# Second block's attention: six of eight head pairs divide by their softmax sums on the finished head rows instead of on the probabilities

## The chip, the cores and the metric

The kernel runs on one core of one Trainium2 chip, as one program. The core's engines each work through their own instruction stream, in order: TensorE (PE: matmuls and transposes; PEld is its weight load), VectorE (DVE), ScalarE (ACT), GpSimd (POOL) and SyncE (SP, which issues DMA). The metric is the time of one execution in microseconds (us), lower is better, as a median of several executions.

## What is computed

Two transformer blocks follow each other, each with two layers, on 512 positions by 1024 features in float32. The change lies in the attention of the second block. Each of its layers has 16 heads of 64 columns: 6 "dilated" ones (kind A), 4 "differential" ones (kind B), 6 "latent" ones (kind C).

```
def causal_attention(q, k, v):                       # kind C
    ...
        s = jnp.einsum('bqhd,bkhd->bhqk', qs, k).astype(jnp.float32) * scale
        p = jax.nn.softmax(jnp.where(causal, s, -jnp.inf), axis=-1)
        return jnp.einsum('bhqk,bkhd->bqhd', p.astype(v.dtype), v)

def diff_attention(q1, q2, k1, k2, v, lam, bias_tab):  # kind B
    ...
        a = probs(q1, k1) - lam * probs(q2, k2)
        return jnp.einsum('bhqk,bkhd->bqhd', a.astype(v.dtype), v)

    # kind A: three dilated windows, mixed by their log-sum-exp
    w = jax.nn.softmax(jnp.stack(lses, axis=0), axis=0)
    o = jnp.sum(w[..., None] * jnp.stack(outs, axis=0).astype(jnp.float32), axis=0)

    o_b = (rms_norm(o_b, subln_g, SUBLN_EPS) * (1.0 - lam_init)).astype(x.dtype)
    heads = jnp.concatenate([o_a.reshape(Bn, S, -1), o_b..., o_c...], axis=-1)
    h = layer_norm(DEEPNORM_ALPHA * x + heads @ w_o, ln1_g, ln1_b)
```

The kernel computes kind A as one softmax over all causal positions with a bias table, which gives the same mixture. So each head is exp(scores) divided by its row sums, times V.

## The kernel before, in words

`second_mix` does one layer's attention in eight units, each a pair of heads, in the order `UNITS`: B0, C0, B1, C1, A0, C2, A1, A2. Every unit has three parts. `proj(i)` projects q, k and v (for kind C from the compressed tiles `ct`; else from the activations `xt`), with three matmuls (L212, L213, L214) for each product, since float32 is split into a high and a low part that the matmul can take. `att()` does the two heads. `fin()`, which before only kind B has, normalises the pair's rows.

The loop at the end of `second_mix` emits `proj(i+1)`, then, in a stretch of raised priority (`AHEAD` = 102), `att()` of unit i and `fin()` of unit i-1. A scheduler sorts all of it into one fixed stream for each engine by these priorities, so that projection matmuls of the next unit stand between the pieces of a head. At run time no engine passes its next instruction.

A head in `att2`: for four blocks of 128 query rows, PE forms scores in PSUM (`sps`, L1025), DVE adds the bias table and finds the row minimum (`L`, `nm`, L1028), ACT takes the exponential and the row sums (L1032). `L` holds the causal parts of the four blocks, 128, 256, 384 and 512 columns wide. Then DVE takes the reciprocal of the four sums (L1041) and multiplies the four parts by it (L1051). `finish()` transposes the probabilities (PE, `tps<-ident,L`, L1063), splits them into `pth` (ACT, L165) and `ptl` (DVE, L169), multiplies by V (PE, `pv`, L1079, L1080, L1077) and puts the result into the pair's rows `heads` (ACT L1089, DVE L1090). In `heads` the partitions are the pair's 128 head columns and the free axis is the 512 positions. V comes from `vpair`: ACT copies the projection (L996), PE transposes it (L999), ACT and DVE split it (L1003, L1004).

Kind B combines two softmaxes on the probabilities (L1053) and divides by the first one's sum at the end: its `fin()` squares the rows (ACT, L1164), sums them (PE, `half2`, L1167), takes the inverse root (POOL, L219, L222), spreads the resulting 128x8 numbers over 128x512 (DVE copy, L1175), transposes that (PE, L1180) and multiplies the rows by it (DVE, L1181).

After the eight units the out-projection multiplies `heads`, split into `ht`, by w_o. A few lines of the pools and of the loop:

```
UNITS = (("B", 0, 3), ("C", 0, 5), ("B", 1, 4), ("C", 1, 6), ("A", 0, 0), ("C", 2, 7), ("A", 1, 1), ("A", 2, 2))
            with self.tc.high_priority(offset=AHEAD):
                for finish in att():
                    finish()
                if fin is not None:
                    fin()
```

Of the kernel before, what the change touches and what calls it, by code (L numbers as in the profile page):

```python
# [9 lines left out]
F32 = mybir.dt.float32  # L10
F32R = mybir.dt.float32r
AF = mybir.ActivationFunctionType
ALU = mybir.AluOpType
# [3 lines left out]
P = 128  # L17
D = 1024
KT = D // P
SEQ = 512  # L20
CTX = 256
NX = SEQ // P
# [95 lines left out]
class _Kernel:  # L118
# [890 lines left out]

    def att2(self, pool, subs, T, V, par, dest, nlam=None, inv=None):  # L1010
        nc = self.nc
        Ps = []
        off = [0, P, 3 * P, 6 * P]
        for _ in subs:
            L = pool.tile([P, 10 * P], F32, tag="L", bufs=3, name="L")
# [23 lines left out]
        L, r = Ps[0]  # L1039
        if nlam is None:  # L1040
            nc.vector.reciprocal(r, r)  # L1041
        else:

            L2, r2 = Ps[1]
            nc.vector.reciprocal(r2, r2)
            nc.vector.scalar_tensor_tensor(r2, r2, nlam, r, op0=ALU.mult, op1=ALU.mult)
            nc.vector.reciprocal(inv, r)
        for i in range(NX):
            c = slice(off[i], off[i] + (i + 1) * P)
            if nlam is None:  # L1050
                nc.vector.tensor_scalar(L[:, c], L[:, c], r[:, i : i + 1], None, ALU.mult)  # L1051
            else:
                nc.vector.scalar_tensor_tensor(  # L1053
                    L[:, c], L2[:, c], r2[:, i : i + 1], L[:, c], op0=ALU.mult, op1=ALU.add
                )
# [38 lines left out]
    def second_mix(self, l, pool):  # L1094
        nc, A = self.nc, self.A
# [18 lines left out]
        nc.vector.tensor_scalar(sg, self.col[:, 102 + l : 103 + l], 1.0 - li, None, ALU.mult)  # L1114

        def dilated(p, o):
            Q, K, L = self.qk(pool), self.qk(pool), self.qk(pool)
# [5 lines left out]
            for j in range(2):  # L1123
# [3 lines left out]
                nc.gpsimd.tensor_copy(K[j][ro], K[j][r])  # L1127
            V = self.vpair(pool, self.proj_t(W, 768 + p * P))

            def att():  # L1130
                for j in range(2):
                    T = self.table(t2, 2 * p + j)
                    yield self.att2(t2, [[(Q[j], K[j]), (Q[j], L[j])]], T, V, j, o)

            return att, None

        def differential(p, o):
# [15 lines left out]
            V = self.vpair(pool, self.proj_t(W, b0 + 512))  # L1153
            inv = self.small(8, "inv", 2)

            def att():
                for j in range(2):
                    T = self.table(t2, 6 + 2 * p + j)
                    subs = [[(QK[0][i], QK[1][i])] for i in (2 * j, 2 * j + 1)]
                    yield self.att2(t2, subs, T, V, j, o, nlam=nlam, inv=inv[:, j:8:2])  # L1160

            def fin():
# [3 lines left out]
                for t in range(NX):  # L1166
# [7 lines left out]
                nc.vector.tensor_tensor(r8, r8, inv, op=ALU.mult)  # L1174
                nc.vector.tensor_copy(  # L1175
                    sq.rearrange("p (a b) -> p a b", b=64), r8.unsqueeze(2).to_broadcast([P, 8, 64])
                )
                tp = self.tps()
                for t in range(NX):
                    nc.tensor.transpose(tp[:, t * P : (t + 1) * P], sq[:, t * P : (t + 1) * P], self.ident)  # L1180
                nc.vector.scalar_tensor_tensor(o, o, sg, tp, op0=ALU.mult, op1=ALU.mult)  # L1181

            return att, fin

        def latent(p, o):
# [10 lines left out]
            for j in range(2):  # L1196
# [8 lines left out]
                qs.append((qh, ql))  # L1205

            def att():
                Tc = self.table(t2, 10)
                for j in range(2):
                    kh, kl = Kb[j]  # L1210
                    qh, ql = qs[j]
                    yield self.att2(t2, [[(qh, kh), (qh, kl), (ql, kh)]], Tc, V, j, o)

            return att, None

# [79 lines left out]
        fin = None  # L1295
        for i in range(len(UNITS)):
# [8 lines left out]
            fin = fn  # L1305
        assert fin is None
        t2.release()
# [189 lines left out]
```

## Time and profile before

| what | value |
|---|---|
| median of 3 runs | 2005.67 us (1997.89 to 2006.74) |
| the profiled execution, its own time | 2004.78 us |
| its span in the trace | 2003.0 us, mean granted PE clock 0.981 |
| PE, DVE, ACT, POOL busy | 1918.2, 1224.4, 895.0, 171.3 us |
| attention stretch of the second block, layer 0 | about 725 to 928 us |
| attention stretch of the second block, layer 1 | about 1350 to 1580 us |

The span is the part of the execution that the trace covers; the other 1.8 us lie around it. Busy shares are over the whole program; the attention stretches have their own, which the rows below show. A line number such as L1051 is the line in the kernel before. Behind the change the same code has other numbers: the transposes L1063 become L1058, the PV matmuls L1079, L1080, L1077 become L1074, L1075, L1072, the row add L1090 becomes L1085, L1167 becomes L1179.

### The profile page before, as it was taken

Reading aid. Unit: us, or ns where it says so; the run is one execution under the profiler, and the core shown is the slowest. Engines: PE = TensorE matmul, PEld = TensorE weight load, DVE = VectorE, ACT = ScalarE, POOL = GpSimd, SP = SyncE. Lnnn points to the kernel's source line nnn. Section 1 sums busy time; section 2 is a strip of 40 time slices with the busy share of each in tenths; the row PEclk is TensorE's granted clock in tenths of the full one; section 3 lists DMA queues with packets and bytes.
Section 4 is the critical chain, followed back from the end, with each engine's and each line's share of the span. In section 5 each row is a group of like instructions: output and inputs, shape, how many; then the busy total and the mean of one; then the engine's idle time right before and its main releaser. Section 6 shows DMA issues by size and latency. Waiting matters only on the chain.

```text
span 2003.0 us, 25662 instructions
## 1 busy us (share of the span) xinstructions
PE 1918.2 (96%) x9516; PEld 1571.8 (78%) x9516; DVE 1224.4 (61%) x2422; ACT 895.0 (45%) x1744; POOL 171.3 (9%) x299
## 2 busy tenths in 40 slices
PE   6999999999999998899999999999899999999997
PEld 4878888788787876777888888887677788888886
DVE  3759984475987668776733434367877673343434
ACT  4746662484654457665321322225756522132220
POOL 2100000030000121101100000012110110000001
PEclk9999999999999999999999999999889999999999
DMA  8414342142432341123432324324112343232421
GB/s 290 151 46 138 102 130 74 44 150 64 127 85 85 119 127 50 53 85 103 124 95 84 107 73 122 95 90 112 48 54 84 108 119 100 78 114 66 126 74 43
DMA packets 220449, 197.19 MB, mean 98 GB/s; under 512 B 30154, under 2 KB 178128, under 8 KB 220324
## 3 DMA queue, kind: packets, MB, share of 16 engines
q1 hardware_dynamic: 209940, 160.32, 27.4%
q0 software_dynamic: 10384, 35.24, 5.3%
q8 instruction: 75, 1.23, 0.3%
q14 instruction: 50, 0.41, 0.1%
HBM read 187.09 MB, written 12.03 MB: 99 GB/s over the span
## 4 chain that ended last, share of the span: by engine, by line
PE 81%; DVE 5%; ACT 5%; issue 2%; DMA 1%; POOL 1%; POOLq 0%; DVEq 0%; ACTq 0%; SPq 0%
PE acc L212 22%; PE acc L213 22%; PE acc L214 22%; PE sps L1025 2%; PE tps L1063 2%; PE tps L792 1%; PE pv L1079 1%; PE pv L803 1%; DVE wl L169 1%; ACT wh L165 1%; ACT L L1032 1%; PE pv L804 1%; PE pv L1080 1%; PE tps L410 1%; DMA wr<-in_w_mod_dram 1%
## 5 line engine op out<-in xcount | busy, mean ns | idle before, releaser
L165 ACT ACTIVATE wh<-wr 128x1024 fp32r<-128x1024 f32 (+3 forms) x299 | 311.7, 1045 | 608.1 <-PE acc L213 266.3
L169 DVE TENSOR_TENSOR wl<-wr,wh 128x1024 fp32r<-128x1024 f32 (+3 forms) x299 | 358.2, 1201 | 256.9 <-ACT wh L165 254.4
L212 PE MATMUL acc<-xt,wh 128*128 128x512 f32 (+1 forms) x1200 | 464.4, 387 | 1.2 <-DVE kb L169 0.7
L214 PE MATMUL acc<-xt,wl 128*128 128x512 f32 (+1 forms) x1200 | 463.7, 386 | 0.0
L213 PE MATMUL acc<-xt,wh 128*128 128x512 f32 (+1 forms) x1200 | 463.0, 386 | 0.0
L212 PEld LDWEIGHTS acc<-xt,wh 128*128 128x128 f32 x1200 | 226.4, 189 | 40.9 <-DVE kb L169 1.1
L214 PEld LDWEIGHTS acc<-xt,wl 128*128 128x128 f32 x1200 | 226.2, 189 | 39.8
L213 PEld LDWEIGHTS acc<-xt,wh 128*128 128x128 f32 x1200 | 226.1, 188 | 38.9 <-issue 0.2
L212 PE MATMUL acc<-wh,ht 128*128 128x512 f32 (+1 forms) x494 | 192.6, 390 | 0.0
L213 PE MATMUL acc<-wl,ht 128*128 128x512 f32 (+1 forms) x494 | 191.8, 388 | 0.0
L214 PE MATMUL acc<-wh,ht 128*128 128x512 f32 (+1 forms) x494 | 191.5, 388 | 0.1
L165 ACT ACTIVATE pth<-tps 128x384 fp32r<-128x384 f32 (+1 forms) x176 | 90.0, 536 | 109.8 <-PE tps L1063 54.3
L169 DVE TENSOR_TENSOR ptl<-tps,pth 128x384 fp32r<-128x384 f32 (+1 forms) x176 | 104.0, 613 | 30.4 <-ACT pth L165 29.6
L214 PEld LDWEIGHTS acc<-wh,ht 128*128 128x128 f32 x494 | 92.9, 188 | 21.8 <-DVE ht L169 1.0
L212 PEld LDWEIGHTS acc<-wh,ht 128*128 128x128 f32 x494 | 92.8, 188 | 20.6
L213 PEld LDWEIGHTS acc<-wl,ht 128*128 128x128 f32 x494 | 92.8, 188 | 20.1
L1418 DVE SCALAR_TENSOR_TENSOR h<-h,acc 128x512 f32<-128x512 f32 (+1 forms) x50 | 33.2, 664 | 114.4 <-PE acc L214 114.4
L1032 ACT ACTIVATE L<-L,nm 128x384 f32<-128x384 f32 (+3 forms) x160 | 88.9, 557 | 24.1 <-DVE nm L1028 23.5
L1384 DVE SCALAR_TENSOR_TENSOR th<-th,acc 128x512 f32<-128x512 f32 x42 | 28.9, 687 | 112.9 <-PE acc L214 112.6
L1028 DVE CUSTOM_DVE_ANT_0 L<-sps,T 128x512 f32<-128x512 f32 (+3 forms) x160 | 74.9, 486 | 26.1 <-PE sps L1025 24.7
L219 POOL TENSOR_SCALAR rv<-bna 128x1 f32<-128x1 f32 x16 | 18.8, 1173 | 792.0 <-DVE bna L1313 792.0
L214 PE MATMUL acc<-wh,xt 128*128 128x256 f32 (+2 forms) x256 | 84.9, 332 | 1.1 <-DVE xt L169 0.8
(315 smaller groups left out, 3390.4 us busy)
## 6 DMA issues: line engine op xcount, KB each, us to landing
wr<-in_w_in_dram SPq DMA_DIRECT2D x66, 512.0 KB, 4.8
wr<-in_w_gate_dram SPq DMA_DIRECT2D x44, 512.0 KB, 4.0
wr<-in_w_up_dram SPq DMA_DIRECT2D x44, 512.0 KB, 4.1
wr<-in_w_down_dram SPq DMA_DIRECT2D x42, 512.0 KB, 3.6
wr<-in_w_mod_dram SPq DMA_DIRECT2D x40, 512.0 KB, 4.5
wr<-in_w_o_dram SPq DMA_DIRECT2D x32, 256.0 KB, 2.7
T<-skew POOLq DMA_DIRECT2D x26, 256.0 KB, 3.1
x<-in_x_dram POOLq DMA_DIRECT2D x8, 512.0 KB, 6.8
```

Of the source, the lines that this page charges most:

```text
L165: self.nc.scalar.activation(out, in_, AF.Copy, scale=scale)
L169: self.nc.vector.tensor_tensor(out, in_, hi.bitcast(F32), op=ALU.subtract)
L212: mm(ps, lh, rh, start=(first and i == 0), stop=False)
L213: mm(ps, lh, rl, start=False, stop=False)
L214: mm(ps, ll, rh, start=False, stop=(last and i == n - 1))
L410: nc.tensor.transpose(v[:, k, :], src[:, (kb * 4 + k) * P : (kb * 4 + k + 1) * P], self.ident)
L1025: nc.tensor.matmul(ps[:, :w], x[:, tok], y[:, :w], start=(k == 0), stop=(k == len(s) - 1))
L1028: nc.vector.tensor_tensor_reduce(lc, ps[:, :n], T[:, SEQ - n : SEQ], 1.0, 3.0e38, op0=ALU.add, op1=ALU.min, accum_out=nm[:, i : i + 1],)
L1032: nc.scalar.activation(lc, lc, AF.Exp, bias=nm[:, i : i + 1], scale=-1.0, accum_out=sums[:, i : i + 1])
L1063: nc.tensor.transpose(tp[:, (i - j) * P : (i - j + 1) * P], L[:, off[i] + j * P : off[i] + (j + 1) * P], self.ident)
L1384: nc.vector.scalar_tensor_tensor(th, th, 0.5, pu, op0=ALU.mult, op1=ALU.mult)
L1418: nc.vector.scalar_tensor_tensor(h[:, c], h[:, c], ALPHA if gi == 0 else 1.0, ps, op0=ALU.mult, op1=ALU.add)
```

## The change

For kinds A and C the four multiplications of the probabilities (L1051) are gone: 4 for each head, 12 heads in a layer, two layers, 96 instructions. The reciprocal stays, and goes into `inv`, 8 columns for a pair. In their place a kind A or C unit gets a `fin()`: `by_row` spreads `inv` over 128x512 (DVE copy, L1113 behind the change), transposes it (four PE transposes, L1118) and multiplies the rows of the pair (DVE, L1120, from PSUM). Kind B calls the same `by_row`, which holds the code that stood in its own `fin()`. The last unit's `fin()` is called behind the loop, without the raised priority. `inv` has three buffers instead of two, and the spread numbers use the pool of `vt`.

```
-    def att2(self, pool, subs, T, V, par, dest, nlam=None, inv=None):
+    def att2(self, pool, subs, T, V, par, dest, inv, nlam=None):
...
-        if nlam is None:
-            nc.vector.reciprocal(r, r)
-        else:
-
+
+        nc.vector.reciprocal(inv, r)
+        if nlam is not None:
             L2, r2 = Ps[1]
             nc.vector.reciprocal(r2, r2)
             nc.vector.scalar_tensor_tensor(r2, r2, nlam, r, op0=ALU.mult, op1=ALU.mult)
-            nc.vector.reciprocal(inv, r)
-        for i in range(NX):
-            c = slice(off[i], off[i] + (i + 1) * P)
-            if nlam is None:
-                nc.vector.tensor_scalar(L[:, c], L[:, c], r[:, i : i + 1], None, ALU.mult)
-            else:
+            for i in range(NX):
+                c = slice(off[i], off[i] + (i + 1) * P)
                 nc.vector.scalar_tensor_tensor(
...
+        def by_row(o, r8, sg, sq):
+
+            nc.vector.tensor_copy(
+                sq.rearrange("p (a b) -> p a b", b=64), r8.unsqueeze(2).to_broadcast([P, 8, 64])
+            )
+            tp = self.tps()
+            for t in range(NX):
+                nc.tensor.transpose(tp[:, t * P : (t + 1) * P], sq[:, t * P : (t + 1) * P], self.ident)
+            if sg is None:
+                nc.vector.tensor_tensor(o, o, tp, op=ALU.mult)
+            else:
+                nc.vector.scalar_tensor_tensor(o, o, sg, tp, op0=ALU.mult, op1=ALU.mult)
...
-            return att, None
+            def fin():
+                by_row(o, inv, None, pool.tile([P, SEQ], F32, tag="vt", bufs=2, name="iv"))
+
+            return att, fin
...
-        assert fin is None
+        fin()
```

The scheduler sorts the streams anew, so more moves than the diff shows. The numbers behind the names are buffers of the built program and differ between the two kernels.

**Layer 0, DVE, the softmax of C0's first head.** `L_7818` holds its exponentials, the `qk` and `wl` rows are other work. Before:

```order
L1041 RECIPROCAL sum5_7820<-sum5_7820 128x4
L169 TENSOR_TENSOR wl_8242<-wr_8239,wh_8241 128x1024
L1051 TENSOR_SCALAR L_7818<-L_7818,sum5_7820 128x128
L171 SCALAR_TENSOR_TENSOR qk_7711<-acc_7684,qk_7711 32x512
L1051 TENSOR_SCALAR L_7818<-L_7818,sum5_7820 128x256
L1051 TENSOR_SCALAR L_7818<-L_7818,sum5_7820 128x384
L1051 TENSOR_SCALAR L_7818<-L_7818,sum5_7820 128x512
L171 SCALAR_TENSOR_TENSOR qk_7712<-acc_7684,qk_7712 32x512
L1028 ISA L_7888,nm5_7889<-sps_7891,T_7816 128x128
```

And with the change (`L_7818` is gone from this place):

```order
L1041 RECIPROCAL inv_7508<-sum5_7821 128x4
L169 TENSOR_TENSOR wl_8244<-wr_8241,wh_8243 128x1024
L171 SCALAR_TENSOR_TENSOR qk_7712<-acc_7685,qk_7712 32x512
L169 TENSOR_TENSOR ptl_7854<-tps_7848,pth_7853 128x512
L169 TENSOR_TENSOR ptl_7862<-tps_7857,pth_7861 128x384
L171 SCALAR_TENSOR_TENSOR qk_7713<-acc_7685,qk_7713 32x512
L1028 ISA L_7885,nm5_7886<-sps_7888,T_7817 128x128
```

The four multiplications have left the row, and the head's splits `ptl_7854` and `ptl_7862` follow at once.

**Layer 0, PE, C0's second head and the scores of B1's second head.** Scores of B1's first head read `qk_7757` to `qk_7758` (behind the change `qk_7758` and `qk_7759`), those of its second head `qk_7759` and `qk_7760` (`qk_7760`, `qk_7761`). `L_7888` and `L_7885` are C0's second head; `vt_7805` and `vt_7806` are B1's V. Before:

```order
L1025 MATMUL sps_8053<-qk_7758,qk_7710 128x384
L1025 MATMUL sps_8060<-qk_7757,qk_7709 128x512
L1025 MATMUL sps_8061<-qk_7758,qk_7710 128x512
L1025 MATMUL sps_8121<-qk_7759,qk_7711 128x256
L1025 MATMUL sps_8122<-qk_7760,qk_7712 128x256
L999 MATMUL acc_7807<-ident_84,vt_7805 128x128 x3
L1063 MATMUL tps_7921<-ident_84,L_7888 128x128
L999 MATMUL acc_7807<-ident_84,vt_7805 128x128
L212 MATMUL acc_7980<-ct_7068,wh_7453 128x512
L213 MATMUL acc_7980<-ct_7069,wh_7453 128x512
```

With the change:

```order
L1025 MATMUL sps_8115<-qk_7760,qk_7712 128x256
L1074 MATMUL pv_7913<-pth_7919,V_7471 128x512
L214 MATMUL acc_7781<-xt_105,wl_7778 128x512
L1025 MATMUL sps_8116<-qk_7761,qk_7713 128x256
L1058 MATMUL tps_7931<-ident_84,L_7885 128x128 x2
L1075 MATMUL pv_7913<-ptl_7920,V_7471 128x512
L1074 MATMUL pv_7913<-pth_7927,V_7471 128x384
L999 MATMUL acc_7808<-ident_84,vt_7806 128x128 x4
L1058 MATMUL tps_7940<-ident_84,L_7885 128x128
L1075 MATMUL pv_7913<-ptl_7928,V_7471 128x384
L1074 MATMUL pv_7913<-pth_7934,V_7471 128x256
```

Before, the last scores of B1's first head and the first of its second stand in one block, and C0's transposes come behind the V transposes. With the change projection matmuls on `xt` stand between the scores, and C0's PV products come ahead of the V transposes.

**Layer 0, PE, B1's `fin()`.** The sums of squares are the `half2` rows, the spread numbers `sq`; `ct` rows are projection matmuls. Before:

```order
L1167 MATMUL tps_8463<-half2_7043,sq_8461 128x2 x4
L999 MATMUL acc_8489<-ident_84,vt_8487 128x128 x4
L212 MATMUL acc_8497<-ct_7068,wh_7453 128x512
L213 MATMUL acc_8497<-ct_7069,wh_7453 128x512
L214 MATMUL acc_8497<-ct_7068,wl_7454 128x512
L212 MATMUL acc_8505<-ct_7064,wh_7438 128x512
L213 MATMUL acc_8505<-ct_7065,wh_7438 128x512
L214 MATMUL acc_8505<-ct_7064,wl_7439 128x512
L212 MATMUL acc_8505<-ct_7066,wh_7446 128x512
L213 MATMUL acc_8505<-ct_7067,wh_7446 128x512
L214 MATMUL acc_8505<-ct_7066,wl_7447 128x512
L1180 MATMUL tps_8477<-ident_84,sq_8461 128x128
```

With the change:

```order
L1179 MATMUL tps_8458<-half2_7043,sq_8456 128x2 x4
L999 MATMUL acc_8484<-ident_84,vt_8482 128x128 x4
L212 MATMUL acc_8492<-ct_7068,wh_7453 128x512
L213 MATMUL acc_8492<-ct_7069,wh_7453 128x512
L1118 MATMUL tps_8472<-ident_84,sq_8456 128x128
L1058 MATMUL tps_8554<-ident_84,L_8529 128x128 x4
L1118 MATMUL tps_8472<-ident_84,sq_8456 128x128 x3
L214 MATMUL acc_8492<-ct_7068,wl_7454 128x512
```

Between the second V transposes and the first transpose of the spread numbers stood nine projection matmuls, and two stand there now; the others come behind.

**Layer 0, the end of the attention, PE.** `ht` rows are the out-projection. Before:

```order
L1079 MATMUL pv_9285<-pth_9306,V_9048 128x256
L1080 MATMUL pv_9285<-ptl_9307,V_9048 128x256
L1077 MATMUL pv_9285<-pth_9314,V_9048 128x128
L212 MATMUL acc_9382<-wh_9351,ht_9328 128x512
L213 MATMUL acc_9382<-wl_9352,ht_9328 128x512
L214 MATMUL acc_9382<-wh_9351,ht_9329 128x512
```

With the change:

```order
L1074 MATMUL pv_9275<-pth_9296,V_9045 128x256
L1118 MATMUL tps_9315<-ident_84,iv_9313 128x128
L1075 MATMUL pv_9275<-ptl_9297,V_9045 128x256
L1072 MATMUL pv_9275<-pth_9304,V_9045 128x128
L1118 MATMUL tps_9315<-ident_84,iv_9313 128x128 x3
L1118 MATMUL tps_9323<-ident_84,iv_9321 128x128 x4
L212 MATMUL acc_9388<-wh_9357,ht_9334 128x512
L213 MATMUL acc_9388<-wl_9358,ht_9334 128x512
L212 MATMUL acc_9422<-wh_9357,ht_9336 128x512
L214 MATMUL acc_9388<-wh_9357,ht_9335 128x512
```

The transposes of the last two units' `inv` (`iv_9313`, `iv_9321`) stand between the last PV products and the out-projection.

**The same place on DVE.** `ht` rows are the splits of the finished rows for the out-projection. Before:

```order
L169 TENSOR_TENSOR ptl_9307<-tps_9303,pth_9306 128x256
L169 TENSOR_TENSOR ht_9329<-heads_7050,ht_9328 128x512
L1090 TENSOR_TENSOR heads_7052<-pv_9285,heads_7052 64x512
L169 TENSOR_TENSOR ht_9331<-heads_7050,ht_9330 128x512
L169 TENSOR_TENSOR ht_9329<-heads_7051,ht_9328 128x256
L169 TENSOR_TENSOR ht_9329<-heads_7052,ht_9328 128x256
```

With the change:

```order
L169 TENSOR_TENSOR ptl_9290<-tps_9285,pth_9289 128x384
L169 TENSOR_TENSOR ptl_9297<-tps_9293,pth_9296 128x256
L1120 TENSOR_TENSOR heads_7052<-heads_7052,tps_9315 128x512
L1085 TENSOR_TENSOR heads_7052<-pv_9275,heads_7052 64x512
L169 TENSOR_TENSOR ht_9335<-heads_7050,ht_9334 128x512
L1120 TENSOR_TENSOR heads_7052<-heads_7052,tps_9323 128x512
L169 TENSOR_TENSOR ht_9337<-heads_7050,ht_9336 128x512
L169 TENSOR_TENSOR ht_9335<-heads_7051,ht_9334 128x256
L169 TENSOR_TENSOR ht_9337<-heads_7051,ht_9336 128x256
L169 TENSOR_TENSOR ht_9335<-heads_7052,ht_9334 128x256
```

The first split of the pairs' rows has moved behind the last row add (L1085), and two multiplications (L1120) have come in.

## Rows read from the trace of the kernel before

**Rows 1.** The page, busy time of each engine, share of the span, instructions.

```profile
PE 1918.2 (96%) x9516; PEld 1571.8 (78%) x9516; DVE 1224.4 (61%) x2422; ACT 895.0 (45%) x1744; POOL 171.3 (9%) x299
```

**Rows 2.** The attention by stretch: us; PE, PEld, DVE, ACT, POOL busy (instructions); PEclk; DMA.

```profile
725.00:928.00 203.00, 183.35 (x892) 141.55 (x891) 159.65 (x399) 135.10 (x322) 35.11 (x54) 0.93 0.26 77
1350.00:1580.00 230.00, 210.46 (x1008) 166.78 (x1007) 176.81 (x445) 148.96 (x355) 41.31 (x68) 0.93 0.30 87
```

**Rows 3.** PE's waits from 725 to 965 us: what it waited for, total, times, longest.

```profile
PE acc L999 <- ACT vt L996: 5.0, 4, 2.3
...
PE acc L212 <- DVE V L1004: 1.4, 1, 1.4
...
PE tps L1063 <- DVE L L1051: 0.9, 3, 0.4
```

**Rows 4.** Shorter stretches, columns as in rows 2.

```profile
784.00:808.00 24.00, 17.46 (x70) 12.85 (x70) 17.41 (x51) 15.62 (x43) 4.06 (x6) 0.73 0.29 77
...
912.00:928.00 16.00, 11.98 (x58) 8.49 (x57) 11.32 (x25) 10.35 (x24) 3.15 (x6) 0.89 0.56 197
...
788.00:792.00 4.00, 2.61 (x8) 1.79 (x8) 4.00 (x15) 2.34 (x6) 0.00 (x0) 0.55 0.93 266
792.00:796.00 4.00, 3.72 (x16) 3.30 (x17) 1.31 (x6) 1.30 (x4) 0.00 (x0) 0.59 0.15 40
...
800.00:804.00 4.00, 1.63 (x4) 0.48 (x2) 2.93 (x10) 3.09 (x9) 1.86 (x2) 0.76 0.00 0
804.00:808.00 4.00, 3.60 (x13) 3.10 (x14) 2.61 (x6) 2.01 (x5) 1.66 (x3) 0.50 0.23 60
```

**Rows 5.** L1051 alone by stretch: us, DVE busy, PEclk, DMA share, GB/s.

```profile
748.00:784.00 36.00, 2.54 (x4) 0.95 0.11 30
784.00:808.00 24.00, 1.35 (x4) 0.73 0.29 77
...
912.00:928.00 16.00, 1.35 (x4) 0.89 0.56 197
sum 203.00, DVE 17.04; mean DVE 2.43
```

**Rows 6.** DVE's groups by line and shape, 725 to 928 us: busy us, mean ns.

```profile
L1090 DVE TENSOR_TENSOR heads<-pv,heads 64x512 f32<-64x512 f32 x16 | 11.0, 688 | 5.5 <-ACT heads L1089 5.2
...
L1051 DVE TENSOR_SCALAR L<-L,sum 128x512 f32<-128x512 f32 x12 | 5.8, 485 | 0.0
...
L1175 DVE COPY sq<-rr 128x512 f32<-128x512 f32 x2 | 1.0, 522 | 0.0
```

**Rows 7.** The transposes of kind B's spread numbers: ns min/median/max.

```profile
L1180 PE MATMUL tps<-ident,sq x16: 272/415/421, 805.4 to 1502.0; 128*128 128x128 f32 x16
```

**Rows 8.** B1's `fin()` in order of time, PE and POOL.

```profile
847.01 1.05 PE L1167 MATMUL tps<-half,sq 128*128 128x2 f32 x8 [1.70 <-ACT sq L1164]
...
849.02 1.67 POOL L222 TENSOR_TENSOR rr<-rv,mhalf 128x8 f32<-128x8 f32 x1
...
849.34 0.40 PE L213 MATMUL acc<-ct,wh 128*128 128x512 f32 x1
849.57 0.39 PE L214 MATMUL acc<-ct,wl 128*128 128x512 f32 x1
...
851.61 0.33 PE L1180 MATMUL tps<-ident,sq 128*128 128x128 f32 x1 [0.97 <-DVE sq L1175]
```

**Rows 9.** The end of the attention in order of time, PE.

```profile
912.26 0.40 PE L214 MATMUL acc<-xt,wl 128*128 128x512 f32 x1
...
915.36 0.60 PE L1063 MATMUL tps<-ident,L 128*128 128x128 f32 x4
915.80 0.42 PE L999 MATMUL acc<-ident,vt 128*128 128x128 f32 x2
...
919.96 0.50 PE L1079 MATMUL pv<-pth,V 128*128 128x512 f32 x1 [1.51 <-DVE V L1004]
...
926.47 0.50 PE L212 MATMUL acc<-wh,ht 128*128 128x512 f32 x1
```

More of the change, by code (lines that the diff above doesn't have):

```diff
@@ L1128, in dilated @@
             V = self.vpair(pool, self.proj_t(W, 768 + p * P))
+            inv = self.small(8, "inv", 3)
             def att():
@@ L1132, in att @@
                     T = self.table(t2, 2 * p + j)
-                    yield self.att2(t2, [[(Q[j], K[j]), (Q[j], L[j])]], T, V, j, o)
-            return att, None
+                    yield self.att2(t2, [[(Q[j], K[j]), (Q[j], L[j])]], T, V, j, o, inv[:, j:8:2])
+            def fin():
+                by_row(o, inv, None, pool.tile([P, SEQ], F32, tag="vt", bufs=2, name="iv"))
+            return att, fin
         def differential(p, o):
@@ L1153, in differential @@
             V = self.vpair(pool, self.proj_t(W, b0 + 512))
-            inv = self.small(8, "inv", 2)
+            inv = self.small(8, "inv", 3)
             def att():
@@ L1159, in att @@
                     subs = [[(QK[0][i], QK[1][i])] for i in (2 * j, 2 * j + 1)]
-                    yield self.att2(t2, subs, T, V, j, o, nlam=nlam, inv=inv[:, j:8:2])
+                    yield self.att2(t2, subs, T, V, j, o, inv[:, j:8:2], nlam=nlam)
             def fin():
@@ L1174, in fin @@
                 nc.vector.tensor_tensor(r8, r8, inv, op=ALU.mult)
[L1175 to L1181, printed above, removed]
+                by_row(o, r8, sg, sq)
             return att, fin
@@ L1205, in latent @@
                 qs.append((qh, ql))
+            inv = self.small(8, "inv", 3)
             def att():
@@ L1211, in att, with fin @@
                     qh, ql = qs[j]
-                    yield self.att2(t2, [[(qh, kh), (qh, kl), (ql, kh)]], Tc, V, j, o)
-            return att, None
+                    yield self.att2(t2, [[(qh, kh), (qh, kl), (ql, kh)]], Tc, V, j, o, inv[:, j:8:2])
+            def fin():
+                by_row(o, inv, None, pool.tile([P, SEQ], F32, tag="vt", bufs=2, name="iv"))
+            return att, fin
         def proj(i):
```

## The prediction

> **What bounds the kernel now.** I began with the page's table of busy time: TensorE is busy for 96% of the span, DVE for 61% [rows 1]. So work taken from DVE shortens the run only where TensorE waits for it, and any TensorE work added is paid in full unless it falls into such a wait. The next view is the busy time by stretch, for the second block's two attentions: PE is busy 183.35 of 203 us in layer 0 and 210.46 of 230 us in layer 1, about 20 us idle in each, and its granted clock averages 0.93 [rows 2]. That idle time, and the time that PE runs at the lower of its two levels (1.2 instead of 2.4 GHz), is all that the change can win back.
>
> Third, PE's waits in layer 0, by what it waited for. The reader is to see how little of them names the line that is removed: 0.9 us for L1051, against 5.0 us for ACT's V copy and 1.4 us for DVE's V split [rows 3]. The direct saving is therefore small. What remains is indirect: L1051 makes DVE late, and DVE makes scores, exponentials and V late.
>
> Fourth, the short stretches show where that happens. From 784 to 808 us PE is busy 17.46 of 24 us, so 6.5 us idle. DVE is full (4.00 of 4) from 788 to 792. The granted clock is 0.55, 0.59, 0.76 and 0.50 in the four stretches listed [rows 4]. Busy time at half clock is time that full clock would not need: 2.61 x 0.45 + 3.72 x 0.41 + 1.63 x 0.24 + 3.60 x 0.50 = 4.9 us. Idle and clock together make 11.4 us in this place per layer. It is the largest target, and layer 1's stretch has the same totals to within 0.2 us of idle and the same mean clock [rows 2], so I work out one layer and double it.
>
> **The change, part by part (per layer).**
>
> *Removed DVE work.* 48 L1051 instructions, 17.0 us by the sum of the stretches [rows 5]. *Added DVE work*: six copies at 0.52 us and six multiplications from PSUM, which the trace before has only as the 64x512 add, 0.69 us [rows 6]; 6 x 1.21 = 7.3 us. DVE gets 9.7 us lighter. I count none of this by itself, since PE sets the end; it enters through the places below.
>
> *Added TensorE work.* Six units times four 128x128 transposes, 24 in all. Four such transposes start at 915.36 and the next instruction starts at 915.80 [rows 9], so 0.11 us apiece when they run in a row at full clock: 24 x 0.11 = **+2.6 us**. Bounds: at half clock twice that, 5.3; a transpose that stands alone shows 0.27 us at least [rows 7], 6.5 in all. I take 2.6, since most stand in threes and fours.
>
> The Trainium skill, page "TensorE: Matmul & The Clock Gate", section "Part 4: PE-mode transpose", speaks against the change here: it gives about 275 ns for a 128x128 transpose inside a kernel. By that figure the 48 transposes of both layers would be an estimated 13.2 us where I have 5.3. The trace agrees for a lone one (272 ns at least) and not for a row of them (0.11 us apart).
>
> *C0's first head.* Its transposes waited 0.9 us for L1051 [rows 3]. Behind the change they wait for the exponential, and the split `ptl` behind them comes next on DVE; I keep 0.3 as a new wait: **-0.6 us** (bounds -0.9 and 0).
>
> *784 to 808 us, C0's second head and the scores of B1.* Ahead of and in this stretch DVE loses 2.54 + 1.35 = 3.9 us of L1051 [rows 5], and nothing of `by_row` for kind C has come yet, as C0's `fin()` belongs to the unit after. So DVE reaches the scores' minimum and the V split at least 3.9 us sooner: that is the lower bound. In the new order scores and projection matmuls alternate where scores stood in a block, so PE has work while DVE catches up; the upper bound is that all 11.4 us go. Nothing in the trace decides between the two, and I take the middle: **-7.6 us**.
>
> *B1's `fin()`.* From the end of the sums of squares (847.01 + 1.05) to the first transpose of the spread numbers (851.61) a chain of DVE, POOL (1.67 us for one operation) and DVE runs for 3.55 us, of which PE waited only 0.97 us, because a V transpose and nine projection matmuls lay in between [rows 8]. Behind the change two of the nine remain. Projection matmuls start 0.23 us apart (849.34 to 849.57), the four V transposes take 0.44: 0.44 + 2 x 0.23 = 0.9 us of cover, so a wait of 2.65 us, 1.7 more. The seven others aren't lost, they run behind it. PE would then be quiet for most of 4 us, with 1.70 us of waiting for the squares just ahead [rows 8]; 1.63 us busy of 4 from 800 to 804 came before a clock of 0.50 [rows 4]. At worst the clock halves for 8 us as from 788 to 796, 2.7 us of loss by the products above; at best it holds. I add 1.7 for it: **+3.4 us** (bounds 1.7 and 4.4).
>
> *The end of the attention.* From the last projection matmul to the out-projection PE needs 14.2 us (912.26 to 926.47) [rows 9], and is idle for 4.0 of 912 to 928 us [rows 4]. 1.51 us of that is the V split [rows 9], which DVE reaches behind 1.35 us of L1051 [rows 5]; that part goes. Of the other 2.5 us of idle time I give back half, since the order puts the pieces of the last but one head in front of the last projection matmuls now, 1.25 us. Against this the first split for the out-projection has moved behind the last row add and stands next to two multiplications of 0.69 us: between 0 and 1.4 us of waiting, I take 0.7. Together **-1.9 us** (bounds -3.9 and +1.4). The eight added transposes are counted already.
>
> *Elsewhere.* Each of the six new `by_row` holds one of two `tps` buffers until its multiplication is done and needs its copy in time; there is no POOL chain in front of it, since `inv` is ready a unit earlier. Kind B's wait of 0.97 us [rows 8] for the same copy is the nearest row, for six: I take **+1.0 us** (bounds 0 and 2.0). The reciprocal only changes its destination, the buffers of `inv` cost nothing, and no DMA is issued anew: SP's stream is the same in the two built programs, and POOL's differs by four copies that have changed places with a neighbour.
>
> *The sum.* 2.6 - 0.6 - 7.6 + 3.4 - 1.9 + 1.0 = -3.1 us per layer, -6.2 us in all. Against the profiled execution's own 2004.78 us this gives **1998.6 us**. (That execution lies 0.9 us below the median of the three runs, so no correction is due.) With the bounds of the largest unknown alone, the stretch from 784 us, the sum goes from +0.6 to -6.9 us per layer: 2006 to 1991. That is the likeliest case's own range.
>
> **The rivals.**
>
> *The waits all go and the clock holds.* The early DVE frees the whole 11.4 us, B1's `fin()` costs only its 1.7, the end gives 3.9: 2.6 - 0.6 - 11.4 + 1.7 - 3.9 + 0.5 = -11.1 us per layer, 1983 us (1976 to 1991). For it: DVE is full right where PE waits. Against it: of PE's 5.0 us for V [rows 3], ACT is the one named, and ACT loses no work.
>
> *TensorE is the bound and the DVE work was covered.* Then the lighter DVE shortens nothing that counts: nothing named L1051 but 0.9 us, the waits of the stretch from 784 us come from ACT and from the order, and they return elsewhere. What is left is transposes: 2 x (2.6 - 0.6) = +4 us, 2009 us; with the lone or the slow price of a transpose, 2 x 5.9 = +12, 2017 us. For it speaks the 96% of PE, against it the full DVE.
>
> *Slower: B0's and B1's `fin()` lose their cover.* Both have the chain of 3.55 us behind the squares. If PE goes quiet at both and the clock falls each time, each costs 1.7 + 2.7 = 4.4 us, and the stretch from 784 us, where B0's lies, keeps only 3.9: 2.6 - 0.6 - 3.9 + 8.8 - 1.9 + 1.0 = +6.0 us per layer, 2017 us (2010 to 2024). It decides from the point where fewer than some ten matmuls stand between squares and spread numbers; for B1 that is so by the order, for B0 it is not (about eleven projection matmuls and four scores stand there), which speaks against this case.
>
> **How the numbers follow.** A measurement of this kernel tells a change from none from about 0.5%, here 10.0 us, so faster is below 1994.8 and slower above 2014.8. Chances: the forecast 0.47 (about 0.20 of it below 1994.8, the rest within), all waits gone 0.19 (0.17 below), TensorE bound 0.20 (0.17 within, 0.03 above), the lost cover 0.14 (0.05 within, 0.09 above). Faster 0.37, same 0.51, slower 0.12. The range for 8 in 10 leaves about one in ten on each side: below 1981 lies half of the first rival, above 2014 most of the last and the tail of the second. 1981 to 2014.
>
> **What would show it.** In the profile after: DVE busy about 19 us less in all and PE about 5 us more at equal clock; four transposes of `iv` within about half a microsecond; the spread copy of B0 well ahead of 804 us and fewer than 6.5 us of idle PE between 784 and 808, with no clock of 0.50 in it; one wait of about 2.6 us in B1's `fin()` ahead of its transposes; an out-projection that starts some 2 us nearer to the last projection matmul. The prediction is wrong if the idle time of PE in an attention stays near 20 us, or if the lower clock moves to another place as long as the one it left.

## The result and the profile after

The changed kernel takes 1981.91 us (median of 4 runs, 1980.19 to 1982.22), the kernel before 2004.52 us; the ratio is 0.9891, with a 95% interval of 0.9866 to 0.9915. That is 22.6 us less. The forecast was 1998.6 us. The first rival's 1983 us is about what was measured; how far its terms were right is told below.

The page of the changed kernel, its busy times (to hold against [rows 1]):

```profile
PE 1901.3 (96%) x9564; PEld 1560.8 (79%) x9564; DVE 1203.6 (61%) x2350; ACT 894.1 (45%) x1744; POOL 169.7 (9%) x299
```

DVE lost 20.8 us and PE has 48 instructions more, as planned; yet PE is busy for 17 us less. Matmuls have not become fewer, so PE ran more of them at its higher clock: the mean granted clock of the whole span rose from 0.981 to 0.993.

To find the place I cut each attention at five events that both kernels have: the first transpose of the latent projections (`xs`), the first `xt` projection matmul behind the setup, the first of A0's projection, the last projection matmul, the first out-projection matmul. The first stretch is the setup (the latent projections' transposes and the matmuls on them, with B0's first scores), then come "B1's scores", "A0 to the last projection" and "the end". The busy times by stretch, kernel before, layer 0 and then layer 1 (columns as in [rows 2]; PEclk is the granted share of the full TensorE clock, 1.00 being the higher of its two levels throughout and 0.50 the lower):

```profile
732.96:749.75 16.79, 12.72 (x52) 8.93 (x50) 12.21 (x32) 12.72 (x30) 3.00 (x5) 0.80 0.22 64
749.75:809.35 59.60, 52.00 (x235) 39.44 (x236) 49.73 (x138) 40.47 (x105) 11.67 (x18) 0.86 0.18 49
809.35:912.26 102.91, 99.04 (x518) 78.83 (x517) 81.60 (x204) 67.34 (x158) 12.70 (x19) 1.00 0.25 72
912.26:926.47 14.21, 10.26 (x52) 7.37 (x50) 9.64 (x20) 8.94 (x20) 2.38 (x5) 0.88 0.63 221
1379.68:1397.20 17.52, 13.03 (x52) 9.20 (x50) 12.30 (x32) 12.93 (x30) 3.01 (x5) 0.81 0.21 60
1397.20:1456.79 59.59, 51.69 (x235) 39.54 (x236) 49.99 (x138) 40.48 (x105) 11.66 (x18) 0.86 0.18 49
1456.79:1561.94 105.15, 102.15 (x518) 81.83 (x516) 81.54 (x203) 67.54 (x158) 12.70 (x19) 0.96 0.23 71
1561.94:1576.40 14.46, 10.45 (x53) 7.61 (x51) 9.64 (x20) 8.94 (x20) 2.39 (x5) 0.88 0.61 219
```

The same view of the changed kernel:

```profile
731.35:746.27 14.92, 10.44 (x52) 7.11 (x50) 12.00 (x32) 12.72 (x30) 3.01 (x5) 1.00 0.25 72
746.27:795.97 49.70, 46.23 (x246) 35.94 (x246) 44.78 (x127) 40.49 (x107) 10.44 (x16) 1.00 0.16 43
795.97:901.76 105.79, 100.63 (x528) 80.96 (x528) 77.19 (x181) 69.20 (x164) 13.61 (x22) 0.98 0.26 79
901.76:914.07 12.31, 8.95 (x55) 6.22 (x53) 8.39 (x16) 7.24 (x16) 0.00 (x0) 1.00 0.22 73
1367.90:1384.92 17.02, 12.89 (x52) 8.93 (x50) 12.30 (x32) 12.90 (x30) 3.00 (x5) 0.80 0.22 63
1384.92:1434.62 49.70, 46.22 (x245) 35.91 (x246) 44.81 (x127) 40.49 (x107) 10.43 (x16) 1.00 0.16 43
1434.62:1540.76 106.14, 100.95 (x527) 81.06 (x528) 77.01 (x181) 69.14 (x164) 13.59 (x22) 0.98 0.26 78
1540.76:1553.05 12.29, 8.95 (x54) 6.20 (x52) 8.38 (x16) 7.24 (x16) 0.00 (x0) 1.00 0.25 79
```

The reader is to see four things. B1's scores take 49.70 us in both layers where they took 59.6: 9.9 us each, the bulk of the gain. Idle time there (length less PE's busy time) went from 7.60 and 7.90 to 3.47 and 3.48 us, and the clock from 0.86 to 1.00. The end is 1.9 and 2.2 us shorter. A0 to the last projection is 2.9 and 1.0 us longer. And the setup, with the same 52 matmuls and 4.1 to 4.5 us of idle time in all four rows, takes 14.92 us at a clock of 1.00 or 16.8 to 17.5 us at 0.80 to 0.81; the change alters no instruction there.

What PE waits for in the changed kernel's first stretch of 49.70 us (to hold against [rows 3]):

```profile
PE acc L212 <- DVE V L1004: 1.0, 1, 1.0
PE acc L212 <- DVE kb L169: 0.8, 2, 0.5
PE acc L999 <- ACT vt L996: 0.8, 2, 0.5
PE acc L212 <- DVE ssb L1184: 0.6, 1, 0.6
```

No wait is longer than 1.0 us. The same stretch of the kernel before:

```profile
PE acc L999 <- ACT vt L996: 3.0, 2, 2.3
PE sps L1025 <- DVE nm L1028: 2.0, 4, 0.9
PE acc L212 <- DVE V L1004: 1.4, 1, 1.4
PE tps L1063 <- DVE L L1051: 0.9, 3, 0.4
PE acc L212 <- DVE kb L169: 0.3, 1, 0.3
```

The longest one was 2.3 us (the V copy), and the clock was 0.55 in the 4 us that hold its end [rows 4]. Two of these waits are all but gone, L1051 itself and the scores' minimum (`nm`), and the V copy's wait fell from 3.0 to 0.8 us.

### The profile page after: what moved, and what is told of

Its sections match the earlier page's. It is cut to its first block, busy times and chain, and to the rows that moved or that the text cites. A ratio compares the mean times of both kernels' runs of the same rounds, so it can differ in the third digit from the quotient of the medians.

```text
span 1979.9 us, 25710 instructions
## 1 busy us (share of the span) xinstructions
PE 1901.3 (96%) x9564; PEld 1560.8 (79%) x9564; DVE 1203.6 (61%) x2350; ACT 894.1 (45%) x1744; POOL 169.7 (9%) x299
## 4 chain that ended last, share of the span: by engine, by line
PE 80%; ACT 6%; DVE 5%; issue 2%; DMA 1%; POOL 1%; POOLq 0%; DVEq 0%; ACTq 0%; SPq 0%
PE acc L212 22%; PE acc L213 22%; PE acc L214 22%; PE sps L1025 2%; PE tps L792 1%; PE tps L1058 1%; ACT wh L165 1%; PE pv L803 1%; PE pv L1074 1%; PE pv L804 1%; DVE wl L169 1%; PE pv L1075 1%; PE tps L410 1%; DMA wr<-in_w_mod_dram 1%; ACT L L1032 1%
## 5 line engine op out<-in xcount | busy, mean ns | idle before, releaser
L1032 ACT ACTIVATE L<-L,nm 128x512 f32<-128x512 f32 (+3 forms) x160 | 89.0, 557 | 31.2 <-DVE nm L1028 29.8
```

The costliest lines, as they stand in the source:

```text
L1032: nc.scalar.activation(lc, lc, AF.Exp, bias=nm[:, i : i + 1], scale=-1.0, accum_out=sums[:, i : i + 1])
```

## The experiments

Theory 1: C0's multiplications make DVE late where PE needs the scores of B1 and its V; without them PE's waits there are short, and PE keeps its clock. Theory 2, the rival: the same waits lower the clock or not depending on the moment at which they come (I call such a fall "a moment" below), and most of the 23 us is such a moment; the setup's rows suggest it. A second rival is that the lighter DVE helps everywhere a little, a third that the new order of the streams does it.

In the table, lengths of the stretches in us, layer 0 / layer 1, are from windows like those above; ratios are to the kernel before on the same chip, with 95% intervals. Beside the twelve runs of the experiments the kernel before itself has medians of 2001.55, 2001.92 and 2005.61 us on three chips, so rows are to be compared by their ratios.

| kernel | median us, ratio | B1's scores | A0 to last projection | end |
|---|---|---|---|---|
| before | 2004.52 | 59.60 / 59.59 | 102.91 / 105.15 | 14.21 / 14.46 |
| changed | 1981.91, 0.9891 (0.9866 to 0.9915) | 49.70 / 49.70 | 105.79 / 106.14 | 12.31 / 12.29 |
| late16 | 2007.53, 1.0030 (1.0016 to 1.0044) | 59.20 / 59.38 | 103.00 / 105.19 | 13.61 / 14.68 |
| late32 | 2007.58, 1.0030 (1.0017 to 1.0044) | 60.24 / 59.59 | 103.36 / 103.04 | 14.63 / 14.19 |
| after_late16 | 1989.86, 0.9944 (0.9922 to 0.9966) | 49.78 / 51.24 | 105.81 / 106.44 | 12.30 / 12.31 |
| no_division | 1979.21, 0.9887 (0.9864 to 0.9910) | 49.70 / 49.78 | 106.75 / 106.65 | 11.29 / 11.21 |
| c_only | 1984.92, 0.9915 (0.9895 to 0.9936) | 49.71 / 49.68 | 104.51 / 104.60 | 13.82 / 13.83 |
| a_only | 2007.74, 1.0027 (1.0014 to 1.0041) | 59.56 / 59.47 | 109.41 / 108.76 | 12.38 / 12.32 |
| both | 2009.26, 1.0039 (1.0027 to 1.0051) | 59.73 / 59.71 | 104.69 / 104.59 | 15.75 / 15.75 |
| c0_only | 1978.48, 0.9872 (0.9856 to 0.9888) | 49.73 / 49.67 | 101.67 / 101.62 | 14.41 / 15.26 |
| act_c0 | 1987.59, 0.9917 (0.9903 to 0.9932) | 50.55 / 55.99 | 104.11 / 104.17 | 14.65 / 14.36 |
| early_root | 1989.95, 0.9943 (0.9924 to 0.9961) | 53.99 / 55.31 | 103.62 / 104.77 | 13.60 / 12.31 |
| early_b1 | 1982.74, 0.9892 (0.9875 to 0.9908) | 51.30 / 49.69 | 105.14 / 104.13 | 13.33 / 12.30 |
| last_old | 1986.36, 0.9912 (0.9897 to 0.9926) | 49.75 / 49.68 | 105.57 / 106.73 | 12.30 / 12.95 |

### Is it the moment?

```
+            tp = self.tps()
+            for _ in range(16):          # late32: 32
+                nc.tensor.transpose(tp[:, 0:P], self.ident, self.ident)
             for l in range(DEPTH):
```

late16: 

> The kernel before with 16 extra transposes of a constant at the start of the second block's first projection (their result is read by nobody); the instruction order of TensorE is otherwise the same. Alone they cost about 16 x 0.11 = 1.8 us. Theory 1 (the change gains because a lighter DVE shortens TensorE's waits, and a TensorE that waits less keeps its clock): nothing here shortens a wait, so 2004.5 + 1.8 = about 2006 us, with about 10 stretches at the lower clock as before. Theory 2 (the same waits lower the clock or not, depending on the moment at which they come; most of the 23 us is such a moment): the time moves by far more than 1.8 us, 5 us or more in either direction, and the stretches at the lower clock come at other places or go.

late32: 

> The same with 32 extra transposes, 3.5 us by themselves. Theory 1: about 2008 us and the same places of lower clock, moved by 3.5 us. Theory 2: a time that differs from 2008 by 5 us or more, and not in line with the run with 16.

after_late16: 

> The changed kernel with the same 16 extra transposes. Theory 1: 1981.9 + 1.8 = about 1984 us; the few stretches at the lower clock stay few (4 or fewer beside the start). Theory 2: it may lose what it gained: 1990 to 2000 us, with the setup's lower clock back.

Both shifted kernels keep B1's scores near 59.6 us in four of four rows, at a clock of 0.86; the shifted change keeps them at 49.78 and 51.24. On the same chip the shifted change is 17.7 us faster than the shifted kernel before (1989.86 and 2007.53). Theory 2 falls for the bulk of the gain.

By the total times alone theory 2 looks better: late16 moved by 6 us (2001.55 to 2007.53) where it said 5 or more, and the shifted change, at 1989.86, came close to its 1990. But the shift was not as clean as planned. PE had to wait before the transposes could start, by the trace for DVE's split of `xt`; late16 first, then late32:

```profile
703.48 0.77 PE L970 MATMUL tps<-ident 128*128 128x128 f32 x5 [1.41 <-DVE xt L169]
702.76 1.42 PE L970 MATMUL tps<-ident 128*128 128x128 f32 x11 [2.02 <-DVE xt L169]
```

So the insertion itself costs 3.1 and 5.5 us rather than the 1.8 and 3.5 of the transposes alone; both runs lost 6 us (0.30%). In the shifted change the wait is 1.95 us. Its span is 7.1 us longer than the change's (1987.0 and 1979.9 us); its two attentions, setup included, take 183.6 and 184.9 us (change: 182.7 and 185.2), so the 7 us lie ahead of them: its setup starts at 738.21 us, the change's at 731.35. About 3.7 us of that is the insertion with its wait. About 1.6 us is there before 550 us already, in work that is the same in both, and most of the rest comes at 650 us, where the clock is at 0.50 from 650.0 to 653.4 us.

The kernel before has a fall of the clock at the same place, in the first block, where the change alters nothing; its rows by stretch, PE alone (us, busy, PEclk, DMA):

```profile
640.00:650.00 10.00, 8.34 (x29) 0.92 0.63 211
650.00:660.00 10.00, 10.00 (x40) 0.91 0.00 1
```

In the changed kernel the clock is 1.00 in both. So 1.6 us of the result (the setup starts at 732.96 and 731.35 us) and up to 2.4 us in the setups are moments, not the change. One more lies inside B1's scores: in layer 0 of the kernel before the clock is 0.50 from 750.9 to 754.3 us, ahead of C0's first L1051 (771.2 us). Those 1.7 us cannot be C0's; layer 1 has no such place, and its stretch is as long.

### What by_row costs, and what the division costs

no_division: 

> Kinds A and C are left undivided altogether: neither L1051 nor by_row; this leaves out the division for 12 of 16 heads. Theory 1: as the changed kernel without its 48 transposes (5.3 us) and the late start of the out-projection: 1973 to 1977 us. Theory 2: waits as short as in the changed kernel, but the time is set by where the clock falls: anything from 1970 to 1990 us.

In it `fin` of kinds A and C is `None` and nothing is divided. B1's scores take 49.70 and 49.78 us. Without the 48 transposes it should have been 5 us faster than the change; it is as fast, within the intervals. The row of its end, PE alone, tells a part of why:

```profile
905.05:916.34 11.29, 8.08 (x33) 0.70 0.64 234
```

The end is only 1.0 us shorter with 22 fewer instructions: the clock is at 0.70 there, where the changed kernel has 1.00. And A0 to the last projection is 1.0 and 0.5 us longer than the change's, at a clock of 0.97 and with nearly as many instructions (525 for 528): work of the last units has moved there from the end.

### Which units, and is it DVE's load?

c_only and a_only put L1051 back for one kind, which then gets no `fin()`; the main lines:

```
+        if div:
+            nc.vector.reciprocal(r, r)
+            ...
+                nc.vector.tensor_scalar(L[:, c], L[:, c], r[:, i : i + 1], None, ALU.mult)
+        else:
+            nc.vector.reciprocal(inv, r)
```

c_only: 

> Only kind C divides at the end; kind A keeps its division on the probabilities (L1051), and nothing is left out. Theory 1 (C0's L1051 makes DVE late just where TensorE waits for the scores of B1): the stretch from the first projection matmul behind the setup to the first one of A0 is 49.7 us as in the changed kernel (before 59.6), the end of the attention stays near 14.3 us; about 2004 - 2 x 9.9 = 1984 us. Rival (the gain is spread over all units, by the lighter DVE as a whole): half of the gain, 1992 to 1995 us.

a_only: 

> Only kind A divides at the end; kind C keeps its L1051, and nothing is left out. Theory 1: the stretch up to A0 stays at 59.6 us, the end of the attention falls to about 12.3 us; 2 x 2 us gained, 1999 to 2003 us. Rival (lighter DVE as a whole): 1992 to 1995 us.

c0_only restricts it to one pair in a layer (`div=p > 0` for kind C, `div=True` for kind A):

> Of the twelve pairs that the change touches only C0, in each layer, divides at the end; the ten others keep L1051. Nothing is left out. Theory 1: C0's 3.9 us of L1051 are the whole cause of the 9.9 us: the stretch up to A0 is 49.7 us, the time 1983 to 1987 us. Rival (C1's and C2's L1051 count too): 1990 us or more.

"both" keeps by_row and puts L1051 back in front of it:

> The changed kernel with L1051 put back on top of by_row, so that kinds A and C divide twice (the output changes accordingly). Theory 1: the stretch up to A0 is back at 59 to 60 us, and by_row's own cost stands alone: 2004 + 2 to 10 = 2006 to 2014 us. Rival (the new order of the streams, by_row's work among it, holds the clock, not the lighter DVE): the stretch stays near 50 us and the time below 1995 us.

In these four kernels the stretch of B1's scores follows C0's L1051: 49.7 us in c_only and c0_only, 59.5 to 59.7 us in a_only and both. The row of c_only, layer 0, PE alone:

```profile
749.61:799.32 49.71, 46.24 (x246) 1.00 0.15 43
```

The same row of a_only:

```profile
746.90:806.46 59.56, 51.67 (x235) 0.86 0.18 49
```

"both" also shows by_row's own cost where the division stays: 15.75 us at the end against 14.2 to 14.5, and 0.39% in all.

What these runs do not separate is load and order. The scheduler lays PE's stream by the load, and in B1's scores it has laid only two streams here: held against each other matmul by matmul in the traces, `both` and a_only run that of the kernel before, c_only, c0_only and no_division that of the change (but for single records that a trace lacks). `both` was to keep the new order under the old load; in this stretch it did not keep it, so it says nothing on the third rival.

Lighter DVE elsewhere gains little or loses: a_only was expected at 1999 to 2003 us and is slower than before by 0.27%, since its 2 us at the end are more than paid back from A0 on (109.41 and 108.76 us). c0_only, with 2 of the 12 pairs changed, has 0.9872 where the change has 0.9891; the intervals overlap, so it is at least as good, and not shown to be better. Against c_only (0.9915) its interval lies wholly lower: dividing C1 and C2 at the end as well made the kernel slower. Held against the change, c0_only's attentions show the trade: they are 4.1 and 4.5 us shorter than the change between A0 and the last projection, and 2.1 and 3.0 us longer at the end.

The streams' order changes along with the load, so I took the load away and meant to keep the order. act_c0 is the kernel before, with C0's multiplications on ACT:

```
-                nc.vector.tensor_scalar(L[:, c], L[:, c], r[:, i : i + 1], None, ALU.mult)
+                if act:
+                    nc.scalar.activation(L[:, c], L[:, c], AF.Copy, scale=r[:, i : i + 1])
```

> The kernel before with C0's eight multiplications (both heads) in each layer done by ACT instead of DVE; no by_row, nothing left out. Theory 1 as stated (DVE's lateness is the cause): most of the gain comes without any by_row, the stretch up to A0 falls to 50 to 54 us, about 1984 to 1993 us. Rival (ACT, full from 784 to 788 us and named for the longest wait there, is as much the limit): the stretch stays at 57 us or more, 1998 to 2006 us.

The block of scores that the prediction spoke of (in the listing ahead of it `sps_8060`, `sps_8061`, `sps_8121`, `sps_8122`, then the V transposes) stands in act_c0's TensorE stream as it stood before. Its rows of B1's scores, PE alone:

```profile
747.18:797.73 50.55, 45.96 (x239) 1.00 0.17 48
...
1386.46:1442.45 55.99, 52.58 (x239) 0.85 0.15 43
```

Idle time is 4.6 and 3.4 us, against 7.6 and 7.9 before. PE's longest waits in layer 0:

```profile
PE acc L212 <- DVE V L1004: 1.8, 1, 1.8
PE sps L1025 <- DVE qk L169: 1.0, 1, 1.0
PE acc L999 <- ACT vt L996: 0.5, 1, 0.5
```

At that block the wait for the V copy fell from 2.3 to 0.5 us with the order as it was, although ACT does more work here: so a lighter DVE queue shortens waits without the new order. But behind the block act_c0 has an order of its own. The last four scores of B1's second head stand in a row in the kernel before (799.71 to 802.21 us) and have other matmuls between them in act_c0 (787.63 to 790.01 us). How much of the rest is load and how much order is not shown.

The clock is another matter: at 3.4 us of idle time it is 0.85 in layer 1, at 4.6 us it is 1.00 in layer 0. The waits just ahead of the place are the same in both layers (0.25 and 1.01 us for DVE in layer 0, 0.26 and 0.99 in layer 1), and only in layer 1 the clock fell, to 0.51 from 1421.57 to 1435.22 us. The smaller idle time there is in part its consequence, since a slower PE comes later to the V split (a wait of 1.05 us for 1.81). The rows of 49.7 us in the table have short waits and a full clock; here short waits did not make the clock certain.

### The loss that is left: B1's fin

In the changed kernel B1's `fin` looks as forecast, PE and POOL in order of time:

```profile
832.87 0.48 PE L212 MATMUL acc<-ct,wh 128*128 128x512 f32 x1
...
833.19 0.40 PE L213 MATMUL acc<-ct,wh 128*128 128x512 f32 x1
833.41 1.67 POOL L222 TENSOR_TENSOR rr<-rv,mhalf 128x8 f32<-128x8 f32 x1
...
835.99 0.33 PE L1118 MATMUL tps<-ident,sq 128*128 128x128 f32 x1 [2.40 <-DVE sq L1113]
...
837.31 0.63 PE L212 MATMUL acc<-ct,wh 128*128 128x512 f32 x1
...
837.73 0.63 PE L213 MATMUL acc<-ct,wh 128*128 128x512 f32 x1
```

Two matmuls of cover, then 2.40 us of waiting (0.97 before [rows 8]), and the matmuls that follow start 0.42 us apart for a few us. early_root issues the squares and the root earlier, and leaves the spreading and the multiplication where they were:

```
                 for finish in att():
                     finish()
+                    if early:
+                        fin, early = fin(), False
```

> The changed kernel with kind B's squares, sums and inverse root issued behind the next unit's first head, and its spreading and multiplication where they were. Theory 1 (B1's fin, with 2.4 us of waiting and 1.7 us of lower clock behind it in each layer, is the largest loss left): 3 to 4 us less per layer, 1974 to 1977 us. Rival (the wait comes back at the next thing that DVE or ACT owe, the V copy): within 2 us of 1982.

The wait goes: A0 to the last projection loses 2.2 and 1.4 us. But B0's chain now stands among B1's scores, where PE waits 2.82 us for a split:

```profile
787.28 0.69 PE L1058 MATMUL tps<-ident,L 128*128 128x128 f32 x2 [2.82 <-DVE ptl L169]
```

The rival was right that a wait would come back, but it came at the split, not at the V copy, and cost more than the "within 2 us" that it gave: the stretch grew by 4.3 and 5.6 us, and the time is 1989.95 us. So I moved B1's chain alone:

early_b1: 

> As the run with the early root, for B1 alone: B0's fin stands where the changed kernel has it. If the lost 4 to 6 us there came from B0's squares among the scores of B1, the stretch up to A0 is back at 49.7 us and the stretch behind it keeps its 3 us of gain: 1975 to 1978 us. If the earlier chain costs as much elsewhere whichever unit it is: 1981 us or more.

1982.74 us where 1975 to 1978 was hoped for, no gain that can be told: the stretches come to 169.8 and 166.1 us from B1's scores to the out-projection (change: 167.8 and 168.1). Layer 1 got its 2 us, layer 0 lost as much, with clocks of 0.97 in B1's scores and 0.87 at the end.

last_old keeps L1051 for A2 (`div=p == 2`) so that nothing stands behind the loop:

> The changed kernel with the last pair, A2, divided on the probabilities as before, so that no fin stands behind the loop. Nothing is left out. If the last pair's transposes and its multiplication ahead of the out-projection cost what the plan priced (0.9 us of transposes, 0.7 us of waiting): the end of the attention is 11.0 to 12 us, 1979 to 1982 us. If its four L1051 in front of the V split cost more: 13 us or more, 1983 us or more.

The ends take 12.30 and 12.95 us, and the ratio is 0.9912 (change: 0.9891): leaving out the fin behind the loop brings nothing back, and the 11 to 12 us and 1979 to 1982 us that my price asked for did not come.

## Why the prediction was right where it was, and where it was not

The time fell, inside the range (1981 to 2014) by 1 us and outside the likeliest case's own range (1991 to 2006). That it lies inside is in part luck, and so is the edge: some 4 us of the gain are clock in places that the change does not touch. The place of the largest term was right and its size was not. The gain is 22.6 us where 6.2 was forecast.

- **784 to 808 us and C0's first head**, forecast -7.6 and -0.6: measured -9.9 in each layer. I took the middle between 3.9 and 11.4 because the trace could not decide; the sum's step "I take the middle" is the one that failed. About 4 of the 9.9 us are idle time; the other 5.8 us are PE's busy time, by my estimate about 7 us of lower clock (52.0 us busy at 0.86) less the 11 instructions that the stretch has gained. L1051's 3.9 us on DVE thus gave about the same in waits, and the clock gave more than that on top. In layer 0, 1.7 of the 9.9 us lie at 750.9 us, ahead of C0's first L1051.
- **The alternation of scores and matmuls**, which I gave for the gain above 3.9 us, is neither shown nor refuted. act_c0 has the old first block and shorter waits, so the alternation there is not needed for them; its second block of scores is broken up as well, and no run kept the old order throughout under the light load.
- **B1's fin**, forecast 2.65 us of waiting: 2.40 us. The clock fell there as priced. But the whole stretch, for which my terms (3.4, twelve of the transposes at 0.11, part of "elsewhere") come to about 5 us, grew by 2.9 and 1.0 us. In layer 1 the kernel before already had a clock of 0.96 here, which my doubling of layer 0 hid.
- **Transposes**: four in a row take 0.36 us (847.52 to 847.88), 0.09 apiece, near the 0.11 used:

```profile
847.52 0.60 PE L1118 MATMUL tps<-ident,iv 128*128 128x128 f32 x4
847.88 0.48 PE L214 MATMUL acc<-xt,wl 128*128 128x512 f32 x1
```

The Trainium skill, page "TensorE: Matmul & The Clock Gate", section "Part 4: PE-mode transpose", gives about 275 ns for one inside a kernel. In this trace that is how long one lasts (271 to 332 ns, median 273), not how far the next start is away.

- **The end**, forecast -1.9 and eight transposes: -1.9 and -2.2 with twelve transposes in it. The size is right by luck. The forecast was made of idle time, and that fell by only 0.6 and 0.7 us (3.95 and 4.01 to 3.36 and 3.34); the wait of 1.51 us for the V split went as forecast, but one of 0.56 us for the out-projection's split came, and the one for the row add grew from 0.42 to 0.93. The rest is the clock, 0.88 to 1.00, and some nine instructions that moved ahead of the last projection matmul (52 instructions before, 55 now with twelve new). From A0 to the out-projection as a whole the change takes 118.1 and 118.4 us, the kernel before 117.1 and 119.6: nothing gained.
- **DVE**, forecast 19.4 us lighter: 20.8. The spread copy takes 0.42 us rather than 0.52.
- **The rival "TensorE is the bound"** is refuted for C0. For kind A it holds: the lighter DVE buys nothing there (a_only).
- **The rival "The waits all go and the clock holds"** has the total and not the terms: it put the stretch at -11.4 and the end at -3.9, against -9.9 and about -2, and B1's `fin()` at 1.7, against some 3.1 in layer 0 (1.43 us more waiting, and 1.7 for a clock of 0.50 from 837.0 to 840.4 us). Without the setup the attentions gained 8.9 and 11.1 us, against its 11.1 in each.
- **Elsewhere**, forecast +1.0 us per layer: PE waits 0.4 us in all, in both layers together, for the copies of `inv`. The term was too high.
- **The setup and the first block**, for which the sum had no term, gave 4 us, by a clock that no step of the change touches.
- **The sign of being wrong** that I named, idle time staying near 20 us in an attention, did not come: from the setup to the out-projection it fell from 19.5 to 16.5 us in layer 0 and from 19.4 to 16.1 in layer 1.

In sum, per layer: setup -1.9 and -0.5, B1's scores -9.9 and -9.9, up to the last projection +2.9 and +1.0, end -1.9 and -2.2; -10.8 and -11.6. With -1.6 ahead of the attentions and +0.8 between and behind them this is, but for rounding, the 23.1 us by which the spans differ (2003.0 and 1979.9).

What stays open: how much of C0's 9.9 us is the lighter DVE itself and how much the order that the scheduler makes of it, and why the clock falls in one layer and not in the other behind equal waits. B1's `fin()` before is a second case of that: PE waits 1.70 us for the squares in layer 0 and 1.67 in layer 1, and the clock stayed at 1.00 in the one and was 0.50 from 1495.0 to 1501.8 us in the other.

## What to carry to other kernels

Take work off an engine that is not the bound only where the bound engine waits for it, and look for that place by stretches: here C0, one pair of the six changed in a layer, carried the whole gain. Price a wait of the matmul engine with the slower clock behind it, which here was worth more than the wait; but take a clock that holds in one run's trace as possible, not as given. Before a chain is moved to an earlier place, look at what is owed there: early_root only exchanged one wait for another.

## What was not expected of the hardware

The setup is the same 52 matmuls with 4.1 to 4.5 us of idle time, and takes 14.92 us at a clock of 1.00 or 16.8 to 18.3 us at 0.72 to 0.81 (c0_only: 18.29 and 16.94 us), with no change in its own work. The whole kernel shows the same from one execution to the next: on one chip 19 executions of the kernel before took 1996.71 to 2006.50 us, the shortest at a mean granted clock of 0.986 and the longest at 0.980. Each trace here is one execution, so a fall of the clock that only one of them shows is weak evidence. The 0.86 of B1's scores is not of that kind: it stands in all ten rows of the five kernels (before, late16, late32, a_only, both) in which DVE does C0's L1051.
